# A hybrid attention encoder block on one core: its opening and its value products set in program order on all engines, six rows of the conditioning weight a piece on VectorE, modulation through PSUM, and two chunks of that weight moved to the branch stage

## The chip, the cores and the metric

The kernel runs on one core of one Trainium2 chip. The metric is the device time of one execution in microseconds (us). TensorE (PE) multiplies matrices, VectorE (DVE), ScalarE (ACT) and GpSimd (POOL) work elementwise, and SyncE (SP) issues nearly all of the DMA transfers, in the order of its queue. Tiles have 128 partitions; SBUF holds operands, and PSUM, in eight banks of 128 x 512 float32, holds what PE writes.

## The reference

One encoder block for a sequence of 1024 positions and model width 1024, conditioned by one vector c. What matters here:

```python
ada = jax.nn.silu(c) @ w_ada[i] + b_ada[i]
shift1, scale1, gate1, shift2, scale2, gate2 = jnp.split(ada, 6, axis=-1)   # 1024 columns each
h = rmsnorm(x, g_mix[i]) * (1 + scale1) + shift1
qa, ka, va, qb, kb, vb, ga, gb = jnp.split(h @ w_in[i], split_at, axis=-1)
oa = mixture_of_dilations(heads(qa), heads(ka), heads(va), rel_bias)
ob = neighbourhood_attention_2d(heads(qb), heads(kb), heads(vb), na_rpb[i])
merged = jax.nn.sigmoid(ga) * (oa @ w_branch_dil[i]) + jax.nn.sigmoid(gb) * (ob @ w_branch_na[i])
x = x + gate1 * (merged @ w_out[i])
h2 = rmsnorm(x, g_ffn[i]) * (1 + scale2) + shift2
...                                   # conv feed-forward network
x = x + gate2 * ((jax.nn.gelu(u_gate) * u_val) @ w_down[i])
```

The weight w_ada is 1024 x 6144 float32 (25 MB). The first 2048 columns (shift1, scale1) are needed before any product with h; gate2, the last 1024, only at the very end.

## The kernel before

Activations lie transposed: a tile of x or h is 128 channels by 512 positions, eight tiles (k = 0..7) for each half hf of the sequence. Every operand of a large product is split into a high and a low part (`split`: ACT writes the high part, DVE or POOL subtracts to get the low), and a product takes three matmuls, high by high, high by low and low by high (lines 77 to 79 for q, k and gates, tile `pj`, 128 x 512; lines 247 to 249 for the values, tile `pv`, 128 x 256).

**The conditioning vector.** w_ada is cut into 12 chunks of 512 columns, each with eight rows of tiles (t = 0..7, 128 x 512), two rows a transfer (512 KB). A chunk's part of `ada` is the sum over t of row t times c's column t, and then over the partitions. The sum over t is done by DVE in place (`ada_rows`, lines 155 and 157: one scaled multiply, then multiply-adds); the sum over partitions is done by PE (`ada_sums`, line 141, tile `pada`: the row is the stationary operand and a column of ones, or of c, the moving one). Chunks 0 to 3 are the four *pieces*: piece q holds the columns of shift1 and scale1 for tiles k = 2q and 2q + 1. Chunks 4 to 11 are called late: 4 and 5 are gate1, 6 to 9 shift2 and scale2, 10 and 11 gate2.

**The opening** is written by hand under `manual_schedule`, so each engine takes the block's instructions in program order. It squares the first half of x and sums over the channels, takes the reciprocal root (`rstd_of`) and spreads it over the partitions with PE transposes (`pbc`). Then the pieces: for each, three or four rows are scaled by ACT and added by POOL (`ada_rows_pool`), the others are done by DVE, `ada_join` adds both, and one row goes to PE as it is. `piece_bias` adds the bias (lines 263 and 265). `scale_x` multiplies x by the reciprocal root, on DVE straight from PSUM or on POOL from a copy in SBUF. `modulate` then writes for each tile the high part by ACT (line 212), the full value by DVE (line 214) and the low part by DVE or POOL (line 215). The products of the first q and k tiles (`qk_products`) and of the first 256 value columns (`v_products`) follow piece by piece. Weights are split with one low on POOL and one on DVE. After the four pieces come the values of columns 256 to 511 for the first half of the sequence, the second half of x in the same way, and chunks 4 and 5.

**The value stage** comes after it and is left to the scheduler, which orders instructions by its own model of time: q and k of the second half, the remaining value steps (`v_product`, 24 matmuls for 128 positions and 256 columns; `v_out` copies the result and stores it), copies of the values into other layouts (`va_chunks`, `vb_chunks`, DRAM to DRAM), and chunks 6 to 11, two after every eight value steps, each through `ada_chunk`: load, eight rows on DVE, a PE sum, the bias. After it the pools of w_ada and the value weights are released, and attention's pool (bias tables, value tiles) takes their space.

**The attention stage** follows, where gates and the next q and k tiles fill PE, and then the **branch stage** (line 794 on, program order): sixteen iterations of 24 matmuls each, for which SP loads a gate tile, a tile of x and the weights, ACT takes the sigmoid, and DVE multiplies, adds and splits. The feed-forward network takes the second half of the time.

Of the kernel before, what the change touches and what calls it, by code (L numbers as in the profile page):

```python
# [9 lines left out]
FT = mybir.dt.float32  # L10
# [18 lines left out]
def hybrid_encoder(tc, xT, c, w_ada, small, w_in, p1_bias, p23_bias, na_bias, ln2_mult, ident, w_br, w_out,  # L29
# [39 lines left out]
    def weights(src, lo_eng):  # L69
        return w_split(w_load(src), lo_eng)  # L70
# [45 lines left out]
    slots = iter(range(1 << 20))  # L116

    def wada_tile(j):
        n = next(slots) if j < 4 else -1
        if n == 0:  # L120
            return qkpool.tile([128, 2, 512], FT, name="kl")
        if n > 0 and (n - 1) % 6 < 2:
            return early.tile([128, 2, 512], FT, name="wada", bufs=2)
        return adapool.tile([128, 2, 512], FT, name="wada", bufs=4)
# [10 lines left out]
    def ada_sums(parts, pa=None, stop=True, n=4):  # L135

        first = pa is None
        pa = ps_s.tile([128, 4], FT, name="pada", bufs=1) if first else pa
# [20 lines left out]
    def ada_rows_pool(wt, ts):  # L159
        for t in ts:  # L160
            act.activation(wt[t], wt[t], AF.Copy, scale=cs[:, t:t + 1])
        for t in ts[1:]:
            pool.tensor_tensor(wt[ts[0]], wt[ts[0]], wt[t], OP.add)

    def ada_join(wt, a, b):
        dve.tensor_tensor(wt[a], wt[a], wt[b], OP.add)

    def ada_chunk(j, wt):
        ada_rows(wt, range(KT))
        ada_bias(4 * j, ada_sums([(wt[0], ones)]))  # L170

    def x_load(hf, ks=range(KT)):
        x = []
        for k in ks:
            x.append(early.tile([128, 512], FT, name="xl", bufs=1) if hf + k == KT else h_tile(FT))
            sp.dma_start(x[-1], xT[k][:, halves[hf]])
        return x
# [4 lines left out]
    def square(x, accs, ks, e):  # L182
        for k in ks:
            acc = accs[k // 4]
            sq = early.tile([128, 512], FT, name="mt", bufs=4) if k % 4 else acc
# [13 lines left out]
    def to_sbuf(pb):  # L199
        bc = early.tile([128, 512], FT, name="mt", bufs=4)  # L200
        act.activation(bc, pb, AF.Copy)
        return bc

    def scale_x(x, pb, bc, ks, e):
        for k in ks:
            e.tensor_tensor(x[k], x[k], pb if e is dve else bc, OP.mult)

    def modulate(x, hf, ks, lo_eng):
        for k in ks:
            a, b = am1[:, k:k + 1], ada[:, k:k + 1]  # L210
            hi, lo = h[hf, k] = h_tile(), h_tile()
            act.activation(hi, x[k], AF.Identity, bias=b, scale=a)  # L212
            t = early.tile([128, 512], FT, name="mt", bufs=4)
            dve.tensor_scalar(t, x[k], a, b, OP.mult, OP.add)
            lo_eng[k % 2].tensor_tensor(lo, t, f(hi), OP.subtract)  # L215
# [4 lines left out]
    v_pools = itertools.cycle((early, work))  # L220

    def v_tiles():
        p = next(v_pools)
        return tuple(p.tile([128, KT, 256], FR, name=n, bufs=1) for n in ("vwh", "vwl"))
# [35 lines left out]
    def piece_bias(q, pa):  # L260

        cc = [t[:, 0:16].rearrange("p (j q i) -> p j q i", j=2, q=4)[:, :, q] for t in (ada, b_ada)]
        dve.tensor_tensor(cc[0], pa.rearrange("p (j i) -> p j i", j=2), cc[1], OP.add)
# [23 lines left out]

    with tc.manual_schedule(engines={e.engine for e in (sp, act, dve, pool, pe)}):
        x = [x_load(0)]
        sp.dma_start(sm, small)  # L290
        wt = {0: ada_load(0)}
        qk_raw = [wpool.tile([128, KT, 128], FT, name="wraw") for _ in range(2)]
        half_load(qk_raw, (0, 4), 0)
        v_raw = [qkpool.tile([128, KT, 128], FT, name="kl") for _ in range(2)]
        half_load(v_raw, (8, 9), 0)
        wt[1] = ada_load(1)
        wt[2] = ada_load(2)
# [25 lines left out]
        for q in range(1, 4):  # L323
# [8 lines left out]
            if q == 1:  # L332
                scale_x(x[0], pb, bc, range(4, 6), pool)
# [1060 lines left out]
```

## Time and profile before

| | |
|---|---|
| time, median of 3 runs | 1579.64 us (1578.32 to 1581.91) |
| the profiled execution's own time | 1584.16 us |
| its span, first to last instruction | 1582.3 us |
| mean granted TensorE clock | 0.98 |
| busy: PE, DVE, ACT, POOL | 1502.5, 1046.1, 815.1, 837.1 us |
| bytes moved by DMA | 196.86 MB, mean 124 GB/s |

Busy time is the time in which an engine executes; DMA issues, waits and branches are not counted. Idle time of an engine that nothing waits for costs nothing, so what matters is which engine ends last in each stage. In the views, a row of groups has the line, the engine, the operation with its output and inputs, the count, the busy time and the mean duration in ns; a row of the timeline has the start and the duration in us and, in brackets, the idle time before it and what ended it ("issue" where nothing that the profile shows was waited for).

### The profile page before, as it was taken

The page shows a single profiled execution, that of the slowest core. Times are in us where ns is not written, and L with a number is a line of the kernel's source. Part 1 is how long each engine was busy: PE and PEld are TensorE (multiplying, and loading weights), DVE is VectorE, ACT ScalarE, POOL GpSimd, SP SyncE. Part 2 cuts the span into 40 slices and gives each one's busy share as a digit, 9 for nine tenths or more (in the row PEclk, how much of TensorE's full clock was granted, in tenths as well). Part 3 has the DMA queues.
Part 4 walks back from the last instruction along what each step waited for, and adds up shares of the span by engine and source line. Part 5 has one row for each costly group of instructions (what it writes and reads, how often), then busy time and mean ns, then how long its engine had stood idle before and what let it go on. Part 6 is the DMA issues. An engine that isn't in the chain of part 4 may idle for free.

```text
span 1582.3 us, 21932 instructions
## 1 busy us (share of the span) xinstructions
PE 1502.5 (95%) x7884; PEld 1284.6 (81%) x7884; DVE 1046.1 (66%) x1872; ACT 815.1 (52%) x1463; POOL 837.1 (53%) x523
## 2 busy tenths in 40 slices
PE   4897989999999999999999899999999999999998
PEld 3797978888888989888888777788888887778788
DVE  6876455676757667544433899876666667887765
ACT  4531165766676677654335354444444446575542
POOL 4562052535344575521246758676666665678711
PEclk9898989999999999999999999999999999999998
DMA  6747832222223344446534212222222223533313
GB/s 230 263 148 276 273 104 69 85 72 79 82 70 120 103 126 132 148 161 226 187 139 160 94 53 80 93 95 80 80 80 82 90 75 141 168 118 122 112 54 107
DMA packets 113268, 196.86 MB, mean 124 GB/s; under 512 B 40072, under 2 KB 61448, under 8 KB 113160
## 3 DMA queue, kind: packets, MB, share of 16 engines
q1 hardware_dynamic: 112888, 195.20, 37.2%
q8 instruction: 62, 1.02, 0.3%
q14 instruction: 46, 0.38, 0.1%
q10 hardware_dynamic: 272, 0.26, 0.1%
HBM read 158.73 MB, written 42.47 MB: 127 GB/s over the span
## 4 chain that ended last, share of the span: by engine, by line
PE 75%; DVE 12%; ACT 4%; issue 3%; DMA 2%; POOL 2%; SPq 1%; DVEq 0%; ACTq 0%; POOLq 0%
PE pj L885 10%; PE pj L886 10%; PE pj L884 10%; PE pj L77 9%; PE pj L78 9%; PE pj L79 9%; PE pj L402 2%; DVE big L1080 2%; PE pv L249 2%; PE pv L247 2%; PE pv L248 2%; PE O L716 2%; PE T L704 1%; PE S L683 1%; PE O L571 1%
## 5 line engine op out<-in xcount | busy, mean ns | idle before, releaser
L56 POOL TENSOR_TENSOR wlo<-wraw,whi 128x1024 fp32r<-128x1024 f32 (+2 forms) x78 | 180.3, 2311 | 273.4 <-ACT whi L55 229.5
L77 PE MATMUL pj<-h,whi 128*128 128x512 f32 x448 | 180.4, 404 | 8.5 <-ACT h L212 6.7
L78 PE MATMUL pj<-h,whi 128*128 128x512 f32 x448 | 180.7, 403 | 2.2 <-DVE h L215 2.1
L79 PE MATMUL pj<-h,wlo 128*128 128x512 f32 x448 | 180.3, 402 | 0.0
L56 POOL TENSOR_TENSOR wsl<-big,wsh 128x1024 fp32r<-128x1024 f32 (+1 forms) x45 | 110.0, 2447 | 47.9 <-ACT wsh L55 47.8
L1080 DVE SCALAR_TENSOR_TENSOR big<-wc,sm,big 128x256 f32<-128x256 f32 (+1 forms) x132 | 119.1, 950 | 17.3 <-ACT big L1074 17.2
L55 ACT ACTIVATE whi<-wraw 128x1024 fp32r<-128x1024 f32 (+2 forms) x81 | 81.2, 1003 | 87.3 <-PE pj L78 45.3
L77 PEld LDWEIGHTS pj<-h,whi 128*128 128x128 f32 x448 | 85.8, 192 | 24.5 <-ACT h L212 7.0
L78 PEld LDWEIGHTS pj<-h,whi 128*128 128x128 f32 x448 | 86.0, 192 | 18.2 <-DVE h L215 3.2
L79 PEld LDWEIGHTS pj<-h,wlo 128*128 128x128 f32 x448 | 85.9, 192 | 15.8
L542 ACT ACTIVATE P<-P,st 128x256 f32<-128x256 f32 x128 | 64.4, 504 | 45.9 <-DVE st L541 45.0
L541 DVE CUSTOM_DVE_ANT_0 P<-S,bias 128x256 f32<-128x256 f32 x128 | 51.8, 421 | 51.4 <-PE S L588 37.3
L157 DVE SCALAR_TENSOR_TENSOR wada<-wada,cs 128x512 f32<-128x512 f32 x67 | 64.9, 969 | 30.5 <-DMA wada<-w_ada 28.5
L429 POOL TENSOR_SCALAR kl<-kl 64x512 fp32r<-64x512 f32 x32 | 63.5, 1983 | 33.1 <-DVE kl L427 30.2
L1080 DVE SCALAR_TENSOR_TENSOR big<-pj,sm,big 128x512 f32<-128x512 f32 x132 | 67.8, 564 | 16.4 <-ACT big L1074 16.4
L1074 ACT ACTIVATE big<-wc,sm 128x512 f32<-128x512 f32 x44 | 35.8, 817 | 76.3 <-DVE wc L897 45.9
L247 PE MATMUL pv<-vwh,h 128*128 128x256 f32 x256 | 74.6, 292 | 0.0
L249 PE MATMUL pv<-vwh,h 128*128 128x256 f32 x256 | 74.4, 291 | 0.0
L248 PE MATMUL pv<-vwl,h 128*128 128x256 f32 x256 | 73.3, 287 | 0.0
L56 POOL TENSOR_TENSOR wsl<-wraw,wsh 128x768 fp32r<-128x768 f32 (+1 forms) x23 | 49.9, 2168 | 43.8 <-ACT wsh L55 43.8
L474 POOL TENSOR_TENSOR vv<-vv 96x256 fp32r<-96x256 f32 (+2 forms) x32 | 41.0, 1292 | 51.9 <-ACT vv L473 47.6
L694 POOL TENSOR_SCALAR P<-P,stb 128x288 f32<-128x288 f32 (+1 forms) x32 | 39.4, 1231 | 53.6 <-DVE stb L691 41.8
(365 smaller groups left out, 4928.2 us busy)
## 6 DMA issues: line engine op xcount, KB each, us to landing
wada<-w_ada SPq DMA_DIRECT2D x47, 512.0 KB, 5.5
wraw<-w_in SPq DMA_DIRECT2D x36, 512.0 KB, 4.3
big<-w_up SPq DMA_DIRECT2D x22, 512.0 KB, 5.2
wraw<-w_up SPq DMA_DIRECT2D x22, 512.0 KB, 3.6
as<-big SPq DMA_DIRECT2D x22, 512.0 KB, 2.9
big<-as SPq DMA_DIRECT2D x22, 512.0 KB, 6.0
wraw<-w_down SPq DMA_DIRECT2D x24, 384.0 KB, 4.2
gs<-gs SPq DMA_DIRECT2D x32, 256.0 KB, 2.0
```

The source lines that it names most:

```text
L55: act.activation(hi, raw, AF.Copy)
L56: lo_eng.tensor_tensor(lo, raw, f(hi), OP.subtract)
L77: pe.matmul(psum, whi[:, k0 + k], mhi, start=k == 0, stop=False)
L78: pe.matmul(psum, whi[:, k0 + k], mlo, start=False, stop=False)
L79: pe.matmul(psum, wlo[:, k0 + k], mhi, start=False, stop=k == n - 1)
L247: pe.matmul(p, hhi, hi[:, k], start=fresh and k == 0, stop=False, skip_group_check=True)
L248: pe.matmul(p, hhi, lo[:, k], start=False, stop=False, skip_group_check=True)
L249: pe.matmul(p, hlo, hi[:, k], start=False, stop=k == KT - 1, skip_group_check=True)
L884: pe.matmul(psum, whi[:, k], bhi, start=j < 4 and k == 0, stop=False, skip_group_check=True)
L885: pe.matmul(psum, whi[:, k], blo, start=False, stop=False, skip_group_check=True)
L886: pe.matmul(psum, wlo[:, k], bhi, start=False, stop=k == n - 1, skip_group_check=True)
L1080: dve.scalar_tensor_tensor(y[:, dst], src, wt, y[:, dst], OP.mult, OP.add)
```

## The change

- *The pieces.* Rows 0 to 5 of each piece are summed by DVE, rows 6 and 7 go to PE with c's columns. `ada_rows_pool`, `ada_join`, `to_sbuf` and `scale_x` go. Both low parts of the q, k and value weights are POOL's.
- *Modulation.* One DVE pass computes x times the gain times the reciprocal root and writes it to a PSUM tile (two, in turn); ACT adds the bias for the high part; a second DVE pass adds the bias and subtracts the high part. All eight tiles of a half use DVE; the tile before is finished after the next is begun.
- *Buffers and loads.* The sixteen transfers of the pieces each get a buffer of their own (`homes`), some in q, k and kl buffers. The second half of x is loaded right behind piece 3.
- *Fillers.* `warm(n, ...)` issues n matmuls of the identity with itself on PE, at seven places of the opening; nothing reads their results.
- *The order.* The block under `manual_schedule` now reaches over q and k of the second half (`qk_steps`, cut by `yield`, q and k in turn for every k) and the first 19 of 24 remaining value steps. Chunks 4 to 9 run through this loop as 24 pairs of rows, seven pairs in flight, with a PE sum every three steps. `va_chunks` and the next weights' loads (`ahead`) have fixed places. Five value steps stay outside.
- *The branch stage.* Chunks 10 and 11 are loaded there, one row of 256 KB an iteration; DVE sums them in a PSUM tile, and PE sums over the partitions at iterations 7 and 15.

The core of the diff:

```diff
-    slots = iter(range(1 << 20))
+    homes = iter([(qkpool, "kl", 3)] + [(qkpool, n, b) for n, b in (("qs", 3), ("ks", 3), ("qb", 2))
+                                        for _ in range((3, 3, 1)[("qs", "ks", "qb").index(n)])]
+                 + [(early, "wada", 3)] * 2 + [(adapool, "wada", 4)] * 4 + [(qkpool, "qb", 2), (early, "wada", 3)])
+    later = itertools.cycle([(adapool, "wada", 4)] * 4 + [(early, "wada", 3)] * 3)
...
-    def modulate(x, hf, ks, lo_eng):
-        for k in ks:
-            a, b = am1[:, k:k + 1], ada[:, k:k + 1]
-            hi, lo = h[hf, k] = h_tile(), h_tile()
-            act.activation(hi, x[k], AF.Identity, bias=b, scale=a)
-            t = early.tile([128, 512], FT, name="mt", bufs=4)
-            dve.tensor_scalar(t, x[k], a, b, OP.mult, OP.add)
-            lo_eng[k % 2].tensor_tensor(lo, t, f(hi), OP.subtract)
+    def modulate(x, hf, ks, pb):
+        last = ()
+        for k in [*ks, None]:
+            if k is not None:
+                hi, lo = h[hf, k] = h_tile(), h_tile()
+                t, b = stage[k % 2], ada[:, k:k + 1]
+                dve.scalar_tensor_tensor(t, x[k], am1[:, k:k + 1], pb, OP.mult, OP.mult)
+                act.activation(hi, t, AF.Identity, bias=b)
+            if last:
+                dve.scalar_tensor_tensor(*last, OP.add, OP.subtract)
+            last = k is not None and (lo, t, b, f(hi))
+
+    def warm(n, dst, fresh=False):
+        for _ in range(n):
+            pe.matmul(dst, idt, idt, start=fresh, stop=False, skip_group_check=True)
...
+        warm(12, first[:, :128], True)
+        accs = sq_accs()
+        square(x[0], accs, range(8), dve)
+        pcol = square_sums(accs)
+        ada_rows(wt[0], range(3))
+        rs = rstd_of(pcol, 4)
+        warm(8, first[:, :128], True)
+        pb = bcast(rs, ps_n, "pbc")
+        ada_rows(wt[0], range(3, 6), wt[0][0])
+        warm(6, first[:, :128], True)
+        pa = ada_sums([(wt[0][t], cs[:, t:t + 1]) for t in (6, 7)], stop=False)
+        ada_sums([(wt[0][0], ones)], pa)
+        warm(6, pa[:, 128:256])
+        stage[0] = ps_n.tile([128, 512], FT, name="pcol")
+        qk_split(0, (pool, pool))
+        v_split(v_raw, (pool, pool), slice(0, 4), v_w[0])
+        pvs = [v_banks()]
+        for q in range(4):
+            ks = range(2 * q, 2 * q + 2)
+            piece_bias(q, pa)
+            modulate(x[0], 0, ks, pb)
+            qk_products(ks)
+            if q < 3:
+                ada_rows(wt[q + 1], range(6))
+            v_products(0, (0, 1), ks)
+            if q == 1:
+                qk_split(1, (pool, pool))
+                v_split(v_raw, (pool, pool), slice(4, 8), v_w[0])
+            if q < 3:
+                pa = ada_sums([(wt[q + 1][t], cs[:, t:t + 1]) for t in (6, 7)], stop=False)
+                ada_sums([(wt[q + 1][0], ones)], pa)
+            v_products(0, (2, 3), ks)
+            if q < 3:
+                warm(4, pa[:, 128:256])
+        v_raw1 = v_load(0, 1)
+        pairs = [(j, i) for j in range(4, 10) for i in range(4)]
+        rows = {n: pair_load(*pairs[n]) for n in range(7)}
+        accs = sq_accs()
+        square(x[1], accs, range(8), dve)
+        v_w.append(v_split(v_raw1, (pool, pool)))
+        steps = qk_steps(0, 0, qk_w, qk_psum)
+        next(steps)
+        next(steps)
+        for st in range(4):
+            v_out(0, 0, st, pvs[0][st])
+        pvs.append(v_banks())
+        v_products(1, (0,), range(8))
+        pcol = square_sums(accs)
+        v_products(1, (1,), range(8))
+        pb = bcast(rstd_of(pcol, 4), ps_n, "pbc")
+        v_products(1, (2, 3), range(8))
+        stage = [ps_n.tile([128, 512], FT, name="pcol"), ps_s.tile([128, 512], FT, name="pv", bufs=3)]
+        modulate(x[1], 1, range(8), pb)
+        for st in range(4):
+            v_out(0, 1, st, pvs[1][st])
+        next(steps)
...
+        for n, (br, hv, st) in enumerate(v_steps[:19]):
+            if n == 4:
+                v_w[1, 0] = v_split(v_raws[0], (pool, pool))
+                v_raws[1] = v_load(1, 1)
+            if n == 6:
+                va_chunks(slice(0, 256))
+            if n == 8:
+                v_w[1, 1] = v_split(v_raws[1], (pool, pool))
+                ahead.update({t: w_load(w_in[t]) for t in (1, 5)})
+            if n == 10:
+                va_chunks(slice(256, 512))
...
+            p = v_product(st, v_w[br, hv])
+            row_pairs(min(24, n * 4 // 3), min(24, (n + 1) * 4 // 3))
+            v_out(br, hv, st, p)
+            if n >= 4 and (n - 4) % 3 == 0 and (n - 4) // 3 < 6:
+                j = 4 + (n - 4) // 3
+                ada_bias(4 * j, ada_sums([(sums.pop(j), ones)]))
+            if n == 18:
+                ada_bias(36, ada_sums([(sums.pop(9), ones)]))
...
+    for br, hv, st in v_steps[19:]:
+        v_out(br, hv, st, v_product(st, v_w[br, hv]))
...
         for i in range(2):
             gate_load(i)
+        row_load(0)
...
+            if i + 1 < 2 * KT:
+                row_load(i + 1)
+            row_add(i)
...
+            if i % 8 == 7:
+                j = late[i][0]
+                ada_bias(4 * j, ada_sums([(sums.pop(j), ones)], new=ps.tile([128, 512], FT, name="pbc")))
```

`row_pairs(n0, n1)` adds the rows of the pairs n0 to n1 - 1 into their chunk's sum on DVE and loads the pair seven further on; `row_load` and `row_add` do the same for single rows in the branch stage, with the buffers of the tile `oraw`.

More of the change, by code (lines that the diff above doesn't have):

```diff
@@ L133, in ada_load, with ada_sums @@
         return rows
-    def ada_sums(parts, pa=None, stop=True, n=4):
+    def ada_sums(parts, pa=None, stop=True, n=4, new=None):
         first = pa is None
-        pa = ps_s.tile([128, 4], FT, name="pada", bufs=1) if first else pa
+        if first:
+            pa = new if new is not None else ps_s.tile([128, 512], FT, name="pada", bufs=1)
         for i, (w, col) in enumerate(parts):
@@ L174, in x_load @@
         for k in ks:
[L175 removed]
+            x.append(h_tile(FT))
             sp.dma_start(x[-1], xT[k][:, halves[hf]])
```

247 lines of the change are left out of this document (103 added, 144 removed).

## The prediction

> **What bounds the kernel now.** The page first: TensorE (PE) is busy nearly everywhere, and the slices with gaps are the first, the second and the fourth. The change lives there and, in small part, in the branch stage.
>
> ```profile
> PE   4897989999999999999999899999999999999998
> PEclk9898989999999999999999999999999999999998
> ```
>
> Each digit is tenths of a fortieth of the span (39.6 us). The second row drops where the first did: after a wait PE also runs slower. Next the waits of PE from 0 to 205 us (engine, line, whom it waited for: us, times, longest).
>
> ```profile
> PE pada L141 <- issue: 12.1, 3, 7.2
> PE S L557 <- DVE st L541: 6.8, 1, 6.8
> PE pj L77 <- ACT h L212: 6.7, 2, 3.8
> ```
>
> The w_ada column sums (pada) wait for rows that VectorE (DVE) has not finished, attention's first scores wait once, and the query products (pj) wait for modulated tiles. The timeline of PE has the places: start, duration, and in brackets the wait before.
>
> ```profile
> 17.29 1.86 PE L141 MATMUL pada<-cs,wada 128*128 128x1 f32 x8 [0.19 <-DMA wada<-w_ada]
> 27.93 0.79 PE L77 MATMUL pj<-h,whi 128*128 128x512 f32 x1 [3.82 <-ACT h L212]
> 30.10 0.63 PE L78 MATMUL pj<-h,whi 128*128 128x512 f32 x1
> 30.53 0.63 PE L79 MATMUL pj<-h,wlo 128*128 128x512 f32 x1
> ...
> 67.39 0.39 PE L77 MATMUL pj<-h,whi 128*128 128x512 f32 x1
> 67.63 0.39 PE L78 MATMUL pj<-h,whi 128*128 128x512 f32 x1
> ...
> 72.33 0.28 PE L247 MATMUL pv<-vwh,h 128*128 128x256 f32 x1
> 72.45 0.28 PE L248 MATMUL pv<-vwl,h 128*128 128x256 f32 x1
> ...
> 129.47 1.83 PE L141 MATMUL pada<-ones,wada 128*128 128x1 f32 x8 [7.20 <-issue]
> ...
> 157.88 1.02 PE L141 MATMUL pada<-ones,wada 128*128 128x1 f32 x8 [1.57 <-issue]
> ...
> 184.80 0.40 PE L77 MATMUL pj<-h,whi 128*128 128x512 f32 x1
> ...
> 203.65 0.58 PE L557 MATMUL S<-ks,qs 128*128 128x256 f32 x1 [6.77 <-DVE st L541]
> ```
>
> Matmul starts lie 0.43 us apart at 30 us and 0.24 apart at 67: half rate and full rate. A value step is 24 matmuls at 0.12 (72.33 to 72.45), 2.9 us; a half of the first q and k is 48 at 0.23, 11.0. At 72.33 the values of columns 256 to 511 begin; the last value step ends at 184.8; attention starts at 203.65.
>
> **The first half.** The DVE timeline prices each piece (a piece is two tiles of h).
>
> ```profile
> 22.11 1.27 DVE L206 TENSOR_TENSOR h<-h,pbc 128x512 f32<-128x512 f32 x2
> 23.31 1.78 DVE L56 TENSOR_TENSOR wlo<-wraw,whi 128x512 fp32r<-128x512 f32 x1
> 25.01 1.75 DVE L56 TENSOR_TENSOR vwl<-kl,vwh 128x512 fp32r<-128x512 f32 x1
> 29.77 0.48 DVE L155 TENSOR_SCALAR wada<-wada,cs 128x512 f32<-128x512 f32 x1
> 30.29 6.71 DVE L157 SCALAR_TENSOR_TENSOR wada<-wada,cs 128x512 f32<-128x512 f32 x4
> 40.64 0.17 DVE L263 TENSOR_TENSOR ada<-pada,sm 128x4 f32<-128x4 f32 x1 [1.97 <-PE pada L141]
> 40.84 0.32 DVE L265 SCALAR_TENSOR_TENSOR am<-ada,sm 128x2 f32<-128x2 f32 x1
> 67.33 0.69 DVE L215 TENSOR_TENSOR h<-mt,h 128x512 fp32r<-128x512 f32 x1
> 109.91 2.33 DVE L157 SCALAR_TENSOR_TENSOR wada<-wada,cs 128x512 f32<-128x512 f32 x3
> ```
>
> A row costs 0.78 us alone (2.33/3) and 1.68 beside GpSimd (POOL) (6.71/4, with this in the POOL timeline):
>
> ```profile
> 29.89 3.20 POOL L163 TENSOR_TENSOR wada<-wada 128x512 f32<-128x512 f32 x2 [3.68 <-ACT wada L161]
> ```
>
> The Trainium skill, page "SBUF — State Buffer", section "Who interferes with whom", says that a DVE instruction with two SBUF inputs and a GpSimd one that reads SBUF exclude each other for a whole instruction, and that DVE with one SBUF input does not meet this. The trace agrees on the first (1.68 against 0.78). By the second the new modulation, with one SBUF and one PSUM input, is free of POOL, and a piece keeps the 9.0 worked out below; were it to clash like a row, its four passes would add up to 3.6. No row here shows which.
>
> Removed: POOL's row sums and scalings, the join, the two DVE weight lows (1.78 and 1.75). Added: six rows on DVE a piece, two row sums on PE. Modulation stays two DVE passes a tile, now through PSUM; its first pass has no row, so it is bounded by 0.64 (1.27/2, an SBUF and a PSUM input) and 0.69, and I take 0.65.
>
> ```profile
> 48.89 0.96 PE L141 MATMUL pada<-ones,wada 128*128 128x1 f32 x8
> 75.16 1.84 PE L91 MATMUL pcol<-ones,sq 128*128 128x1 f32 x16
> 79.78 0.60 PE L104 MATMUL pbc<-idt,rs 128*128 128x128 f32 x4
> 65.22 1.52 ACT L212 ACTIVATE h<-h,ada,am 128x512 fp32r<-128x512 f32 x2 [7.24 <-DVE am L265]
> 66.65 2.00 ACT L55 ACTIVATE vwh<-wraw 128x1024 fp32r<-128x1024 f32 x2
> 69.59 1.14 ACT L186 ACTIVATE mt<-h 128x512 f32<-128x512 f32 x2
> L56 POOL TENSOR_TENSOR vwl<-wraw,vwh 128x1024 fp32r<-128x1024 f32 x5 | 12.9, 2606 | 31.5 <-ACT vwh L55 31.5
> ```
>
> First product: piece 0 has landed by 17.3. PE then has fourteen filler matmuls and four transposes (0.15 to 0.3 each by the 0.60 row, full and half rate) and three sums of eight (0.96 to 1.86). From about 15.3 that ends between 21 and 26; bias 0.5, first pass 0.65, ScalarE (ACT) 0.76 and 0.3 of signalling put the first product at 23 to 28. I take 25.3: 2.6 before 27.93, or nothing at the far end.
>
> A later piece: rows 0.48 + 5 x 0.78 = 4.4; sum 0.96 and 0.1; bias 0.5; modulation 3.0 (four passes at 0.65 and a wait on ACT's 0.76). That is 9.0, three times. The second half of the weights is split by POOL during the third piece's rows: four rows at 1.68 instead of 0.78 add 3.6. The first piece's modulation ends on DVE two passes after the first product, at 26.7; 26.7 + 9.0 + 12.6 + 9.0 = 57.3, and ACT's last tile of the half is ready 0.7 before, at **A = 56.6**, against 66.7 (65.22 + 1.52). Bounds: no clash, A = 53; all fifteen later scaled rows clashing, A = 66.4.
>
> **What takes the place of that.** In ACT's new order the eight squares of the second half (8 x 0.57 = 4.6) come before the split of the second value weights, whose two lows are now both POOL's. The lows are ready at A + 4.6 + 1.0 + 2 x 2.6 = A + 10.8. PE has only 5.6 us of products left at A - 0.8, so it idles some 6 us, and values 256 to 511 begin at 67.4 instead of 72.33: 4.9 gained of the 10. The 7.20 wait shows what comes after such a pause: 2.7 us lost at half rate. The Trainium skill, "TensorE: Matmul & The Clock Gate", section "HAM oscillation — how this bites in real kernels", names idle gaps over about 3.4 us as the point; this trace agrees at 7.20.
>
> **To the end of the values.** PE work from there is the same list for both kernels: 11.5 + 1.8 + 0.6 + 11.0 + 24 steps x 2.87 = 68.9. That is 93.8, plus eight sums before (7.7) and six after (5.8). Before: 72.33 + 93.8 + 7.7 = 173.8, and 7.20 + 1.57 + 2.7 make 185.3: the trace has 184.8. So the waits in this stretch are all there is to win. They come from late rows:
>
> ```profile
> 127.83 1.54 DVE L157 SCALAR_TENSOR_TENSOR wada<-wada,cs 128x512 f32<-128x512 f32 x2 [4.91 <-DMA wada<-w_ada]
> 150.00:160.00 10.00, 8.43 (x71) 8.26 (x70) 7.72 (x10) 2.10 (x4) 2.51 (x2) 1.00 1.00 348
> ```
>
> The change has seven pairs in flight, so a single late one no longer stops PE. But 24 pairs over 17 value steps ask for 12.6 MB in 55 us beside 4 to 6 MB of stores, copies and weights, while the window row shows the DMA engines full at 348 GB/s. PE meets DVE in program order, so a late pair reaches it. The loads ahead of it are lighter: 15 MB to A are 270 GB/s, and no piece waits for a buffer any more, so I cost them at nothing. For the pairs I charge 2 us, bounds 0 and 8 (the two waits of before). DVE is covered: 42 rows at 0.78 and six at 0.48 are 36 us, some 15 more beside POOL, in 59 of PE. After: 67.4 + 2.7 + 93.8 + 5.8 + 2 = 171.7: **13.1** before 184.8 (4.9 - 2.7 + 11.5 - 2 + 1.9 - rounding of 0.5).
>
> **Entry to attention.** The wait of 6.77 hangs on bias tables, which are loaded after the value copies on SP's queue, as the chain of work that ended last has it:
>
> ```profile
> 183.66 4.57 DMA vbc<-vs
> ...
> 197.19 4.82 DMA bias<-p_bias
> ```
>
> In the change the buffers of w_ada, whose space the tables take, are free five value steps (14 us) before the last store, so the tables can land under values and the 48 products that now fill 184.8 to 197. I take **6.8** gained; the other bound is 0.
>
> **Branch stage.** Sixteen rows of 256 KB, one an iteration, and two sums.
>
> ```profile
> 742.47 0.69 DVE L821 TENSOR_TENSOR g<-pj,g 128x512 f32<-128x512 f32 x1
> 745.21 0.70 DVE L822 TENSOR_TENSOR pj<-pj,g 128x512 f32<-128x512 f32 x1 [2.06 <-PE pj L79]
> ```
>
> DVE idles 2.06 us an iteration, and a row of 0.78 fits. What stays is PE's two sums, 2 x 0.96: **1.9** lost. On SP row_load(0) waits for a buffer of the last oraw splits and holds the gates and w_br behind it; six PSUM banks (three iterations) cover that, else 2 to 4 us.
>
> **The sum:** 13.1 + 6.8 - 1.9 = 18. The profiled execution took 1584.16 (span 1582.3), so about 1566 there; the median of the runs is 4.5 lower, 1579.64, so **1561**.
>
> **Rivals.**
> - More. Rows never clash (A = 53: 3.6), pairs are in time (2), and the half rate after 203.65 goes too (2.7): 26, **1553**. For it: POOL is idle in most of the pieces.
> - The entry wait stays, because value copies still precede the tables on SP: 11, **1568**. For it: the same queue and the same copies.
> - The clock does not hold between pieces. A cycle's PE work (12 x 0.23 + 24 x 0.12 + 3 x 0.96 = 8.5, fillers 1) is some 15 to 17 at half rate, with the DVE part that it can't cover about 13, and A goes to 67 or so: some 8 gained, **1571**. Against it: products, sums and fillers leave no gap over 3 us.
> - Slower: the port. If DVE's rows clash with POOL throughout, A is 66.4 and the 48 rows of the value stage take about 78 us from A + 41, so they end at A + 119 and the values at A + 134 = 200: 16 later than 184.8, with 6.8 - 1.9 given back: 11 lost, **1591**. It turns the sign when all eleven more in the pieces (10 us) and over thirty of the 42 in the value stage clash, since PE's work covers about 23 of those at 0.9 each. For it: all lows are POOL's now. Against it: after its first four splits POOL has four more of 1.7 in the pieces, and in the 59 us of the value stage four of 2.6 and the q and k copies. The Trainium skill's rule of exclusion, cited above, is this rival's mechanism.
>
> **How the numbers follow.** Forecast 0.36; more 0.18; entry wait stays 0.19; clock 0.07; port 0.15; losses and gains cancel 0.05. A measurement of this kernel tells about 0.2% (3.2 us) from no change. Faster: 0.36 + 0.18 + 0.19 + 0.07 = 0.80; same 0.05; slower 0.15. The range reaches from below the better case to above the clock case, 1546 to 1576, leaving out the port and the cancelling case; the forecast's own is 1556 to 1566.
>
> **What would show it.** Right: last ACT tile of the first half at 54 to 59; a PE wait of about 6 us before the values of columns 256 to 511, with POOL as releaser; last value step near 172; no wait over 2 us before attention's first score; a branch stage longer by about 2. Wrong: row instructions of 1.6 us all through the value stage, waits before the pada sums adding to over 8, or a score that still waits for bias.

## The result, and the profile after

The changed kernel is slower: 1590.69 us, median of 12 runs (1585.19 to 1598.98), against 1580.96 for the kernel before (12 runs, 1577.71 to 1586.59); the ratio is 1.0068, with a 95% interval of 1.0049 to 1.0087. The prediction was 1561. The profiled execution is the fastest of the twelve, 1585.19 (span 1583.4); before's took 1584.16. So the two traces differ by 1 us where the medians differ by 10: stages can be compared, the sum of the stages less so.

The page's slices, PE's busy share and granted clock:

```profile
PE   7799899999999999998999889999999999899998
PEclk8899999999999999999999999999999999999999
```

The first slice is fuller than before (7 for 4), and the fourth too (9 for 7); the second is emptier (7 for 8). The fuller slices are fillers and other work on PE, not an earlier end, as the waits of PE from 0 to 205 us say (engine, line, whom it waited for: us, times, longest):

```profile
PE pj L79 <- ACT h L201: 7.8, 4, 2.0
PE S L588 <- DVE st L572: 6.2, 1, 6.2
...
PE T L595 <- ACT P L573: 2.7, 1, 2.7
PE pv L239 <- POOL vwl L56: 2.7, 1, 2.7
...
PE pada L148 <- DVE wada L164: 1.3, 1, 1.3
```

The 12.1 us of waiting for late rows are gone but for 1.3, as predicted. The wait for scores is still there (6.2 for 6.8), with one for transposes behind it, and the products wait at each of the four pieces. The timeline of PE has those places (start, duration, in brackets the wait before):

```profile
25.56 0.50 PE L79 MATMUL pj<-h,whi 128*128 128x512 f32 x1 [1.96 <-ACT h L201]
37.50 0.49 PE L79 MATMUL pj<-h,whi 128*128 128x512 f32 x1 [1.96 <-ACT h L201]
53.98 0.50 PE L79 MATMUL pj<-h,whi 128*128 128x512 f32 x1 [1.96 <-ACT h L201]
67.48 0.51 PE L79 MATMUL pj<-h,whi 128*128 128x512 f32 x1 [1.96 <-ACT h L201]
78.24 0.39 PE L239 MATMUL pv<-vwl,h 128*128 128x256 f32 x1 [2.68 <-POOL vwl L56]
...
196.44 0.58 PE L588 MATMUL S<-ks,qs 128*128 128x256 f32 x1 [6.22 <-DVE st L572]
200.35 0.97 PE L595 MATMUL T<-idt,P 128*128 128x128 f32 x2 [2.69 <-ACT P L573]
...
717.38 0.78 PE L79 MATMUL pj<-o0hi,whi 128*128 128x512 f32 x1 [4.46 <-ACT gs L763]
```

The pieces begin at 25.56, 37.50, 53.98 and 67.48: cycles of 11.9, 16.5 and 13.5 us. What sets them is seen on DVE, where the bias of a piece (L254, the first step of its modulation) waits for `pada`, the tile of the sums, which fills one bank of PSUM:

```profile
26.93 0.48 DVE L162 TENSOR_SCALAR ks<-ks,cs 128x512 f32<-128x512 f32 x1
27.44 3.90 DVE L164 SCALAR_TENSOR_TENSOR ks<-ks,cs 128x512 f32<-128x512 f32 x5
35.57 0.16 DVE L254 TENSOR_TENSOR ada<-pada,sm 128x4 f32<-128x4 f32 x1 [4.23 <-PE pada L209]
38.81 1.47 DVE L162 TENSOR_SCALAR wada<-wada,cs 128x512 f32<-128x512 f32 x1
40.31 6.61 DVE L164 SCALAR_TENSOR_TENSOR wada<-wada,cs 128x512 f32<-128x512 f32 x5
52.05 0.16 DVE L254 TENSOR_TENSOR ada<-pada,sm 128x4 f32<-128x4 f32 x1 [5.13 <-PE pada L209]
58.16 1.54 DVE L164 SCALAR_TENSOR_TENSOR wada<-qb,cs,wada 128x512 f32<-128x512 f32 x2
65.56 0.16 DVE L254 TENSOR_TENSOR ada<-pada,sm 128x4 f32<-128x4 f32 x1 [5.86 <-PE pada L209]
```

The releaser is L209, the fillers: `warm(4, pa[:, 128:256])` writes the tile that the bias reads, though other columns of it, and PE reaches it only behind the values that stand after the sums. From the last row to the bias are 4.2 us, 5.1 and 5.9.

At the entry to attention SP issues the tables behind the last value store, and POOL adds the mask to them after that:

```profile
189.59 0.53 SPq L246 DMA_DIRECT2D vbc<-vs  x1
190.22 0.38 SPq L769 DMA_DIRECT2D lnm<-ln_mult  x1
190.65 0.45 SPq L560 DMA_DIRECT2D bias<-p_bias  x1
...
194.93 0.99 POOL L562 TENSOR_TENSOR bias<-bias,lnm 128x384 f32<-128x384 f32 x1 [1.37 <-DMA bias<-p_bias]
```

And ahead of the branch stage, on ACT:

```profile
714.58 1.32 ACT L55 ACTIVATE o1hi<-oraw 128x512 fp32r<-128x512 f32 x2 [4.41 <-DMA oraw<-ob]
715.80 1.04 ACT L55 ACTIVATE whi<-wraw 128x1024 fp32r<-128x1024 f32 x1
716.75 0.58 ACT L763 ACTIVATE gs<-pj 128x512 f32<-128x512 f32 x1
```

Two splits of the second branch's operand wait 4.41 us for their load, and behind them in ACT's queue stand a branch weight and the last gate copy, for which PE waits 4.46 us. PE met no such wait before: the gate copy stood ahead of those splits, as the kernel before's ACT shows:

```profile
718.53 0.58 ACT L732 ACTIVATE gs<-pj 128x512 f32<-128x512 f32 x1
720.15 1.25 ACT L55 ACTIVATE o1hi<-oraw 128x512 fp32r<-128x512 f32 x2 [1.04 <-DMA oraw<-ob]
```

By stage, in the profiled runs (us from the span's start). "Scores" is where PE starts on the attention stage proper; "first x" is where SP issues the store of the first x tile behind the branch stage; "last x" is where it has issued the last store of an x tile:

| kernel | scores | first x | last x |
|---|---|---|---|
| before | 203.65 | 811.91 | 1574.76 |
| after | 196.44 | 815.26 | 1575.90 |

After is 7.2 ahead at the scores and 3.4 behind at the first x tile.

### The profile page after: what moved, and what is told of

Its sections match the earlier page's. It is cut to its first block, busy times and chain, and to the rows that moved or that the text cites. A ratio compares the mean times of both kernels' runs of the same rounds, so it can differ in the third digit from the quotient of the medians.

```text
span 1583.4 us, 22101 instructions
## 1 busy us (share of the span) xinstructions
PE 1514.5 (96%) x8012; PEld 1295.8 (82%) x8012; DVE 1030.1 (65%) x1870; ACT 804.6 (51%) x1447; POOL 807.9 (51%) x504
## 5 line engine op out<-in xcount | busy, mean ns | idle before, releaser
L55 ACT ACTIVATE wsh<-big 128x1024 fp32r<-128x1024 f32 (+1 forms) x45 | 44.9, 1001 | 38.3 <-POOL big L906 23.8
L1163 ACT ACTIVATE big<-big 128x1024 f32<-128x1024 f32 x22 | 23.3, 1060 | 80.0 <-DVE big L1137 80.0
```

The lines of the kernel that those rows point to most:

```text
L55: act.activation(hi, raw, AF.Copy)
```

## The experiments

Every time below is compared with the kernel before on the same chip; its median there is given where the runs are first told of. The stages behind the first x tile, whose code is the same in all kernels, took 760 to 767 us in the 14 profiled runs, so a difference of a few us between two single profiles cannot be placed there.

### The parts alone

**The fillers out of the sums' bank.**

```diff
-        warm(6, pa[:, 128:256])
...
-            if q < 3:
-                warm(4, pa[:, 128:256])
```

> The change without the fillers that write into the pada tile (six after the first piece's sums, four before each later bias); the other fillers stay. In the profile of the change the four bias adds on DVE wait 21.6 us in all for the filler line, and the last tile of the first half is ready at 68 us. Theory A (the fillers stand in the chain: a bias waits for the whole pada tile, so for the value products and fillers queued behind the sums): each later piece becomes shorter by the 1.6 of value products and the 1.0 to 1.9 of fillers, the last ACT tile of the half comes at 58 to 60 us, and the time falls by 5 to 8 us below the change's 1590.7, to about 1584. Rival B (the fillers keep PE at full rate): without them the products of the pieces run at half rate, the last tile stays at 66 us or later, and the time stays within 2 us of 1590.7 or rises.

Measured: 1592.01 us (1586.11 to 1595.76), ratio 1.0070 (1.0051 to 1.0089); before 1581.08. No gain. But the opening did what the first theory said: the last piece began at 59.42 (67.48 in after), and the value stage 6.8 us earlier. PE then stood longer at the scores, 9.14 us, and came to the first x tile at 815.0, where after had 815.26. In this run a gain ahead of attention was worth nothing while the tables came late. Of the 4.5 us by which this kernel's scores were still earlier (191.97), attention gave back 3.2 and the branch entry 1.0; the waits on PE explain little of the first, and I leave it open. The bias still waits, now for the sums themselves (L148):

```profile
33.62 0.16 DVE L254 TENSOR_TENSOR ada<-pada,sm 128x4 f32<-128x4 f32 x1 [3.17 <-PE pada L148]
46.53 0.16 DVE L254 TENSOR_TENSOR ada<-pada,sm 128x4 f32<-128x4 f32 x1 [1.58 <-PE pada L148]
57.49 0.16 DVE L254 TENSOR_TENSOR ada<-pada,sm 128x4 f32<-128x4 f32 x1 [3.32 <-PE pada L148]
```

So the fillers' place is 1.1, 3.6 and 2.5 us of the three waits in after, and the rest is work that PE has ahead of the sums.

**The branch part alone, on the kernel before.**

```diff
-                if jj < 12:
+                if jj < 10:
...
+        row_load(0)
...
+            if i + 1 < 2 * KT:
+                row_load(i + 1)
+            row_add(i)
...
+            if i % 8 == 7:
+                j = late[i][0]
+                ada_bias(4 * j, ada_sums([(sums.pop(j), ones)], new=ps.tile([128, 512], FT, name="pbc")))
```

> The kernel before with the branch part of the change alone: chunks 10 and 11 in the branch stage, nothing else. Theory A (the branch part loses by itself: the copy of the last gate result stands on ACT behind splits that wait for attention's last output, PE waits 4.5 us and then loses 1.8 us at half rate, and the two sums cost 1.9): 6 to 8 us slower than before, near 1588, with that wait in the profile and value products ending 2 us earlier. Rival B (the loss comes with the new opening and value stage and the branch part only shows it): within 2 us of before, 1579 to 1583, no wait over 1 us before the first branch products.

Measured: 1577.46 (1573.1 to 1580.99), ratio 0.9977 (0.9965 to 0.9990): faster than the kernel before, which I had not expected. With two chunks less in the value stage SP issues the tables at 172.01, ahead of the last value stores, and the scores follow the values without a wait (first row: the kernel before; the others: this run):

```profile
196.70 0.44 SPq L529 DMA_DIRECT2D bias<-p_bias  x1
...
172.01 0.46 SPq L530 DMA_DIRECT2D bias<-p_bias  x1
...
182.30 0.28 PE L558 MATMUL S<-ks,qs 128*128 128x256 f32 x1
...
707.91 0.80 PE L77 MATMUL pj<-o0hi,whi 128*128 128x512 f32 x1 [4.27 <-ACT gs L733]
```

At 182.30 some 48 products are still to be done that before had behind it at 203.65 (11.3 us), so the real lead is 10 us; attention adds 4 to it, for which I have no cause. The branch stage takes 9 back: the wait of 4.27, 2.7 of half rate after it (192 products in 46.84 us, before 44.10), 1.9 of sums. First x is 5.1 earlier (806.84). So the part that I had priced at 1.9 lost is worth 10 in one place and costs 9 in another.

**The rest alone**: after with chunks 10 and 11 taken behind the last value step, and before's branch stage.

```diff
+    for j in (10, 11):
+        wt = ada_load(j)
+        ada_rows(wt, range(KT))
+        ada_bias(4 * j, ada_sums([(wt[0], ones)]))
...
-            if i + 1 < 2 * KT:
-                row_load(i + 1)
-            row_add(i)
```

> The change without its branch part: chunks 10 and 11 are summed after the last value step, as before; opening and value stage are the change's. Theory A (branch part 8 us of loss, opening and value stage a small gain): 5 to 8 us faster than the change, 1583 to 1585, so still slower than before by 2 or 3, or equal; PE goes into the branch stage without a wait. Rival B (the opening and value stage lose in most executions, and the one that was profiled is the lucky one): within 3 us of 1590.7, with the loss somewhere between 0 and 700 us in its profile.

Measured: 1580.24 (1571.16 to 1589.39), ratio 0.9991 (0.9973 to 1.0010). The new opening and value stage alone are worth nothing that can be told from zero, and both parts together cost 10 us: they do not add up. The spread is the widest of all kernels. The profiled run had a granted clock of 0.59 from 40 to 60 us, where after's had 0.79, and its scores began at 210.58; it was the slowest of the twelve.

### The branch entry

**Late rows in a buffer of their own**, in after.

```diff
-            rows[n] = opool.tile([128, 512], FT, name="oraw", bufs=4)
+            rows[n] = work.tile([128, 512], FT, name="rw", bufs=1)
```

> The change with the late rows of w_ada in a buffer of their own (one of 2 KB a partition) instead of the ring of the last attention outputs. Theory A (the ring makes the first late row wait for the splits of those outputs, the loads behind it on SP wait too, and ACT gets them in an order that holds the last gate copy): the 4.5 us wait before the first branch products goes, and the 1.8 us at half rate with it; 5 to 7 us faster than the change, about 1585. Rival B (the wait belongs to the gates or to the DMA whatever the buffer): the same wait, 1590 or so.

Measured: 1591.22 (1589.75 to 1595.43), ratio 1.0070 (1.0056 to 1.0084): no gain. One operand split still stands ahead of the gate copy, waits 3.95 us, and PE waits 4.23. The ring was not the reason.

**The first late load moved behind the weight**, on the kernel before with the branch part, and on after.

```diff
-        row_load(0)
         ws[0] = w_split(w_raw[0], pool)
...
+            if i == 0:
+                row_load(0)
             if i + 1 < 2 * KT:
                 row_load(i + 1)
```

> Before plus the branch part alone, with one line moved: the load of the first late row of w_ada is issued in the first iteration of the branch loop, behind the split of the first branch weight, not ahead of it. In the kernel with the branch part alone ScalarE held two operand splits, which waited 4.46 us for a load, ahead of the first branch weight and the last gate copy, and TensorE stood 4.27 us before the first branch product, then ran its next products at half rate (192 in 46.84 us where 45.0 is the full rate). Theory A, that order costs the branch stage its time: the wait goes, the stage loses only the two sums (1.9 us), and the time is 1577.46 - 6.1 = 1571 us (1569 to 1574). Rival B, the work ahead of the wait is late anyway and another wait takes its place: 1576 to 1579 us.

> After with the same line moved. Theory A: the wait of 4.46 us at the branch entry and 1.8 us of half rate go: 1590.7 - 6.3 = 1584.4 us (1582 to 1587). Rival B: no gain, 1589 to 1592 us.

Measured, with before at 1580.12: on the kernel before 1573.27 (1568.65 to 1576.65), ratio 0.9948 (0.9929 to 0.9967); on after 1588.72 (1582.96 to 1594.82), ratio 1.0048 (1.0029 to 1.0067). PE in the first and in the second:

```profile
702.11 0.50 PE L77 MATMUL pj<-o0hi,whi 128*128 128x512 f32 x1 [1.45 <-ACT gs L733]
720.53 0.50 PE L79 MATMUL pj<-o0hi,whi 128*128 128x512 f32 x1 [1.45 <-ACT gs L763]
```

ACT takes the weight (the second branch weight, by its place behind the gates' sigmoids, not the first as I had written) and the gate copy before the five operand splits again, the wait falls from 4.3 or 4.5 us to 1.45, and the next 192 products run at full rate (44.22 us; 46.84 and 45.81). That is 5.4 us saved on PE in the kernel before and 0.29% (4.6 us) of its time; in after it is 4.6 us on PE and 0.20% of the time, between the two theories, whose numbers the intervals do not part there, nor is 0.20% told from nothing. The order on ACT is the scheduler's, and one transfer that is written a few lines earlier changes it: that much is shown. Why its model puts it so is not.

### What holds up the gain

**Three things mended in after**: the moved line, no fillers in the sums' bank, and the first head's table loaded inside the value stage.

```diff
+            if n == 12:
+                lnm = entry.tile([128, 384], FT, name="lnm")
+                sp.dma_start(lnm, ln2_mult)
+                bt0 = entry.tile([128, 896], FT, name="bias", bufs=1)
+                sp.dma_start(bt0[:, 0:512], p1_bias[0])
+                sp.dma_start(bt0[:, 512:896], p23_bias[0])
+            if n == 16:
+                pool.tensor_tensor(bt0[:, 512:896], bt0[:, 512:896], lnm, OP.add)
...
+            if head == 0:
+                bt = bt0
...
+    bias_pools = itertools.cycle((sm_pool, entry))
...
-    later = itertools.cycle([(adapool, "wada", 4)] * 4 + [(early, "wada", 3)] * 3)
+    later = itertools.cycle([(adapool, "wada", 4)] * 4 + [(early, "wada", 2)] * 2)
```

> After with three things mended at once: the line of the branch part moved as in the two kernels above, the fillers into the pada bank left out, and the causal-bias table of the first head with its mask loaded and added inside the value stage, in a tile of its own (TensorE waited 6.22 us before the first scores for that chain; to make room six pairs of w_ada rows are ahead where seven were, and the bias tiles alternate between two pools). Theory A, the three waits add up: 1590.7 - 6.3 (branch entry) - 6.8 (the value stage began 6.8 us earlier without the fillers) - 4 (the entry wait without the 2 us that the rest of the chain holds) = 1573.6 us (1570 to 1578). Rival B, the attention stage gives back what is gained ahead of it, as it did for the kernel without the fillers: only the branch entry's gain is left, 1583 to 1587 us.

Measured: 1565.02 (1563.69 to 1567.08), ratio 0.9897 (0.9878 to 0.9916): 26 us faster than after, 16 faster than before, and more than the three waits added up. The timeline of PE:

```profile
59.80 0.50 PE L79 MATMUL pj<-h,whi 128*128 128x512 f32 x1 [0.43 <-ACT h L202]
70.52 0.58 PE L240 MATMUL pv<-vwl,h 128*128 128x256 f32 x1 [3.62 <-POOL vwl L56]
...
186.95 0.28 PE L598 MATMUL S<-ks,qs 128*128 128x256 f32 x1
...
698.33 0.51 PE L79 MATMUL pj<-o0hi,whi 128*128 128x512 f32 x1 [1.61 <-ACT gs L773]
```

The scores begin without a wait.

**The square of two edits.** With the moved line in all four: the table without the fillers' removal, and the removal without the table.

> The kernel with three things mended, with the fillers put back into the pada bank: so after with the moved line and the first head's bias table loaded early. With after with the moved line alone (1588.72 us), the kernel with three things mended (1565.02) and the next run it makes a square of two edits. Theory A, the two add: the bias table is worth 4 to 8 us and the fillers' absence 16 to 20, so 1581 to 1585 us. Rival B, the table alone holds the attention stage up (the kernel without the fillers came to the first scores earlier and won nothing): the fillers are worth nothing or little until it is there, and the table alone brings most, 1570 to 1576 us.

> The kernel with three things mended without the early bias table: after with the moved line and without the fillers. Theory A, the two add: 1588.72 minus 16 to 20 is 1569 to 1573 us. Rival B, what is gained ahead of the attention stage waits there for the bias table, as in the kernel without the fillers alone (9.14 us of waiting before the first scores where after had 6.22): 1584 to 1588 us.

Measured, ratios to before (1582.51 for the two new ones):

| | fillers behind the sums | no fillers |
|---|---|---|
| table as in after | 1.0048 (1588.72) | 1.0009 (1585.51; 0.9993 to 1.0026) |
| table early | 0.9984 (1580.70; 0.9968 to 1.0000) | 0.9897 (1565.02) |

The early table is worth 0.64% (10 us) with the fillers and 1.12% (18 us) without; the fillers' absence 0.39% (6 us) without the table and 0.87% (14 us) with it. Each edit brings more once the other is there, so neither theory has it whole: they add, and 8 us more (0.48%, by my estimate some 0.35% either way, from the four intervals). Where the table is late, its wait takes part of what the opening gains:

```profile
191.02 0.58 PE L585 MATMUL S<-ks,qs 128*128 128x256 f32 x1 [8.67 <-DVE st L569]
194.72 0.97 PE L592 MATMUL T<-idt,P 128*128 128x128 f32 x2 [2.48 <-ACT P L570]
```

**The fillers kept, but ahead of the row sum**, in the kernel with three things mended.

```diff
+        warm(6, pa[:, 128:256])
         ada_sums([(wt[0][0], ones)], pa)
...
+                warm(4, pa[:, 128:256])
                 ada_sums([(wt[q + 1][0], ones)], pa)
```

> The kernel with three things mended, with all 18 fillers of the pada bank put back, but each group ahead of the product of the row sum, not behind it: they are out of the way of the values and of the bias as far as the order on TensorE goes, though the bias still reads a bank that they write. Theory A, the fillers cost time only because the bias waits for what stands behind the sum in its bank: 1565 to 1568 us. Rival B, it is their presence (TensorE's time, the granted clock) that costs: 1575 to 1581 us, as with the fillers behind the sum (0.9984 of before against 0.9897).

Measured: 1567.94 (1565.76 to 1569.53), ratio 0.9917 (0.9899 to 0.9935); before 1581.68. Behind the sums the same 18 fillers cost 14 us, ahead of them 3, which the intervals do not part from nothing. What costs is their place, as the first theory said: behind the sums the bias waits for them. The last piece's bias, with the fillers behind the sums (the table early in both) and ahead of them:

```profile
66.28 0.16 DVE L255 TENSOR_TENSOR ada<-pada,sm 128x4 f32<-128x4 f32 x1 [5.92 <-PE pada L210]
...
59.34 0.16 DVE L255 TENSOR_TENSOR ada<-pada,sm 128x4 f32<-128x4 f32 x1 [3.54 <-PE pada L149]
```

The scores come at 191.13 and 184.30. The granted clock from 20 to 80 us is the same in the two (0.88 and 0.89 in the mean), so there the wait parts them and not the clock.

**The first head's table late again**, with the bias tiles in two pools as in the kernel with three things mended.

```diff
-            if n == 12:
-                lnm = entry.tile([128, 384], FT, name="lnm")
-                sp.dma_start(lnm, ln2_mult)
...
+            if n == 18:
+                pool.memset(entry.tile([128, 896], FT, name="bias", bufs=1)[:, :8], 0.0)
...
-            if head == 0:
-                bt = bt0
...
             bt = next(bias_pools).tile([128, 896], FT, name="bias", bufs=1)
```

> The kernel with three things mended, with the first head's bias table and the mask loaded where after loads them, behind the last value step, while the bias tiles still alternate between two pools and six pairs are ahead: only the early load is taken back (the second head's table now comes early, since its tile is free). Theory A, the early load of the first table is what shortens the entry and the attention stage: the 6 to 9 us of waiting before the first scores come back, and the time is that of the kernel without the table, 1580 to 1586 us. Rival B, the tiles in two pools do it, by the waits that they spare inside the attention stage: 1566 to 1572 us.

Measured: 1576.01 (1573.05 to 1579.01), ratio 0.9969 (0.9957 to 0.9981). Between the theories: of the 1.12% that came with the table 0.72% (11 us) hang on the early load and 0.40% (6 us) on what came with it to make room, the tiles in two pools and the second head's table, which is early here. The memset only takes the turn of the early table in its pool. The wait is back:

```profile
189.99 0.58 PE L590 MATMUL S<-ks,qs 128*128 128x256 f32 x1 [8.32 <-DVE st L574]
```

**The low halves of the second value weights on VectorE and GpSimd**, in the kernel with three things mended.

```diff
-        v_w.append(v_split(v_raw1, (pool, pool)))
+        v_w.append(v_split(v_raw1, (dve, pool)))
```

> The kernel with three things mended, with the low halves of the second value weights split on VectorE and GpSimd, as before had them, where both were on GpSimd. TensorE waited 3.62 us there for the second of the two (2.44 us each, one after the other). Theory A: that wait falls by about 2.4 us and the gain passes on to the end: 1565.0 - 2.4 = 1562.6 us (1561 to 1564.5). Rival B, VectorE's q and k splits, which then stand behind the low half, hold TensorE or the second half's squares instead: 1564.5 to 1567 us.

Measured: 1566.68 (1562.92 to 1568.65), ratio 0.9895 (0.9873 to 0.9916). No difference. The wait fell only from 3.62 to 2.45 us, and the first x tile came 2.4 us earlier (792.37 for 794.74), but the profiled run gave that back behind it, in code that is the same.

## Why the prediction was wrong, by its steps

**The first product** came at 25.56, predicted 25.3, and that is partly luck. The bias ahead of it also waits for fillers in its tile (6.42 us, L209), which the sum did not count; in the run without them it is 24.67. And the same opening had it at 27.99 and 28.98 in two other profiled runs (the rest alone, and after with the moved line).

**The piece cycle is the step that failed first.** It had 9.0, 12.6 and 9.0, and A (the half's last tile ready on ACT) at 56.6; the trace has 11.9, 16.5 and 13.5, and the last ACT tile of the half ready at 68.1 (67.40 + 0.69). The terms: rows 4.4, measured 4.4 (0.48 + 3.90); the third piece's clash 3.6, measured 3.7 (8.1 for 4.4); modulation 3.0, measured 2.9 (65.95 to 68.87 on DVE). The one that was mis-sized is "sum 0.96 and 0.1; bias 0.5". Between the last row and the bias stood the sums of three groups (24 matmuls, 2.73 us in the first piece), twelve value products and the fillers, 4.2 to 5.9 us in all. I had counted PE's fillers as work and not asked what they write: the tile that the bias waits for. Without them the last piece began 8 us earlier. Their place alone is worth 11 us of time where the first table is early (0.9984 against 0.9917, 0.67%), some 7 of them at the scores; in after itself, where the table is late, taking them out brought nothing. The rest of the term, 3.2, 1.6 and 3.3 us for the sums and the values ahead of them where I had 1.1, was in no run taken away.

**The wait for the second value weights** was predicted at 6 us, with POOL as releaser, and measured at 2.68. The mechanism is right; it is shorter mostly because PE's products before it took 8.1 us (67.48 to 75.56, part of them at half rate) where I had 5.6. The place, 67.4, became 78.24, which is A's delay.

**To the end of the values** the sum was right: the waits for late rows went, and what I charged for late pairs (2 us) came to 1.1 for stores. In my order of work the last value step ends at 186.09 less the 30 products that now lie before it (7.1), 179.0; predicted 171.7. A had cost 10.8 at the second value weights, of which 3.5 came back, in part from what I had charged for half rate and late pairs. So this part gained 5.8, not 13.1. (The 2.7 us at half rate behind the kernel before's wait of 7.20 were a little small: its rows give 3.2, from 26 value products at 0.21 for 0.12 and eight sums in 1.69 us for 0.92.)

**The entry to attention** is the second step that failed: 6.8 gained was the wrong one of the two bounds, and the rival "the entry wait stays" had the mechanism. Freed space for the tables did not bring them forward; they stayed behind the last value store in SP's queue. The early load of the table takes the wait away and, without the fillers, is worth 11 us. That is more than the wait: the two profiled runs place only 3.8 us ahead of the first x tile (798.56 and 794.74), and where the rest lies is open.

**The branch stage** is the third: 1.9 predicted, 8.0 measured from PE's last product ahead of it to the first x tile (102.3 us, before 94.4): 4.46 of waiting, 1.7 of half rate (192 products in 45.81 us, before 44.10), 1.9 of sums. I had named row_load(0) and 2 to 4 us and then called it covered by six PSUM banks. It is not: the first product waits for the last gate copy, and ACT takes that copy after the splits. Moving row_load(0) alone gave 0.29% back in the kernel before with the branch part.

**What the sum left out** is that taking two chunks from the value stage was by itself the best part of the change: 10 us at the scores. I had credited that stretch to the new value loop.

**From the sum to the median.** By its steps the prediction had 18 us gained; by the steps as measured 5.8 + 0.5 - 2.7 - 8.0 is 4.4 lost (2.7 is the new wait of the transposes), and the first x tile is 3.4 late. The median says 9.7 lost. The rest is in the runs: the profiled one is after's fastest, 5.5 us below its median, where before's is 3.2 above its own. After's granted clock goes, loosely, with time from run to run (0.980 in that one, 0.969 to 0.975 in the four of 1595 to 1599 us; the kernel before's 23 runs beside the first experiments lie at 0.977 to 0.985). Of after itself only the fastest run was profiled; the windows of the first pieces of after, and of the same opening in after with the moved line (1589.26 us), suggest where (busy times by engine, then PEclk, DMA share, GB/s):

```profile
20.00:40.00 20.00, 15.50 (x105) 13.74 (x105) 11.62 (x19) 4.62 (x8) 3.88 (x5) 0.95 1.03 401
60.00:80.00 20.00, 15.08 (x97) 13.47 (x96) 9.97 (x16) 10.78 (x18) 6.55 (x4) 0.89 0.30 117
...
20.00:40.00 20.00, 18.04 (x111) 16.31 (x111) 7.36 (x12) 2.00 (x3) 3.63 (x3) 0.74 1.03 401
60.00:80.00 20.00, 17.75 (x97) 15.30 (x97) 11.52 (x19) 7.81 (x13) 1.28 (x1) 0.80 0.37 132
```

At 0.74 and 0.80 the same code begins its last piece at 72.93, where it was 67.48 at 0.95 and 0.89. So the rival "the clock does not hold between pieces" (0.07) is probably part of the answer, and I had held against it that no gap is over 3 us.

**The port** was not it, though its number, 1591, is the one measured: that is chance. Rows clash with POOL in one piece of the three, as forecast, and of the 48 in the value stage five took 1.9 to 2.8 us and 42 no more than 0.78; they add up to 44 us where that rival had 78, and PE waited for none.

The kernel with three things mended, 1565, lies within 4 us of the number predicted for the change. That bears out what the change could have been worth, not how I came by it.

## What to carry to other kernels

Ask of every added instruction what it writes, not only what it costs: a filler in the tile of a result made the reader wait for the filler and for all that stood before it on its engine. Before a gain is booked, follow it to the next thing that comes at a fixed time, here a table at the end of one DMA queue; two edits on the two sides of that point were worth more together than one by one, so test such a pair as a square. And look at the order that a scheduler gives the neighbouring stage: one transfer written a few lines too early cost the branch stage some 5 us.

## What the runs showed of the hardware

In this trace the clock falls after gaps much shorter than I had allowed for, though not after each: three of the four waits of 1.96 us at the pieces were followed by half rate within 2 us, and the one at 25.56 was not (1.00 from 26 to 30 us). After the wait at 37.50 the granted clock of after is 0.54 and 0.60 for the next 4 us:

```profile
36.00:38.00 2.00, 0.49 (x1) 0.19 (x1) 1.90 (x3) 1.24 (x2) 0.00 (x0) 1.00 1.04 389
38.00:40.00 2.00, 1.71 (x4) 1.43 (x5) 2.00 (x3) 2.00 (x5) 1.30 (x2) 0.54 1.06 389
40.00:42.00 2.00, 2.00 (x7) 1.53 (x7) 1.93 (x3) 0.18 (x1) 2.00 (x2) 0.60 1.05 392
42.00:44.00 2.00, 2.00 (x18) 1.90 (x16) 1.96 (x2) 0.00 (x0) 2.00 (x2) 1.00 0.97 370
```

The Trainium skill, page "TensorE: Matmul & The Clock Gate", section "HAM oscillation — how this bites in real kernels", puts the point at gaps of some 3.4 us; this trace does not agree, at 1.96.

A scaled row with one tile as input (L162) took 1.47 us beside POOL and 0.48 alone (55.28), three times as long; the row with two inputs 1.32 (6.61/5) and 0.78. So the prediction was too wide where it took a DVE instruction with one SBUF input to be free of POOL. The modulation's passes, with one input in PSUM, took 0.74 to 0.76 each; POOL was idle beside nearly all of them, so whether they would clash is still not shown.
